# Gate and up in a macaron block: four pairs by seven products in every column group, the plain banks added by transfers, silu held back

## The chip, the cores and the metric

One core of one Trainium2 chip runs one program. The metric is device time in microseconds, from the start to the end of one execution; a kernel's time is the median of its runs. A profiled execution gives the trace: when each instruction began on each engine, how long it took and what it waited for. TensorE (PE) multiplies, VectorE (DVE) and ScalarE (ACT) work on what it reads and writes, GpSimd (POOL) issues a few transfers here, and SyncE (SP) issues the weight loads.

## The reference

The kernel computes one layer of a streaming encoder on x of 256 frames by 2048 channels, in float32. The two feed-forward half steps are where the change lies:

```python
D_MODEL = 2048; SEQ = 256; D_FF = 5504

def swiglu(h, w_gate, w_up, w_down):
    return (jax.nn.silu(h @ w_gate) * (h @ w_up)) @ w_down
...
x = x + 1/2 * SwiGLU_1(RMSNorm(x))
x = x + mixing(RMSNorm(x))     # gated DeltaNet and chunked attention, untouched here
x = x + 1/2 * SwiGLU_2(RMSNorm(x))
```

## The kernel before

**Precision.** A float32 product is made of three matmuls on halves in the type fp32r: a number is a high half (a rounded copy) plus a low half (the difference). `product` issues high by high (L455), high by low (L456) and low by high (L457) into one PSUM bank. ScalarE makes high halves by a cast, VectorE makes low halves by a subtraction.

**Column groups.** The 5504 columns of gate and up are 43 blocks of 128, taken as eleven groups of four blocks (the last has three). The groups form chunks, `CHUNKS = ((0, 4), (4, 8), (8, 11))`: after the groups of a chunk, the down projection of its blocks runs (names pd, L606 to L640). A group is named after its first block: `f1_8` is group 2 of the first feed-forward, and its banks are `pf1_8_b`. In the second feed-forward the program's names have f3, and the text calls its groups by the same numbers.

**Pairs.** The 2048 rows of a weight are 16 blocks, so eight pairs. One weight item holds one pair of gate and up columns: two 512 KB loads into a `raw` tile. A *plain* pair needs eight products, 24 matmuls: ScalarE casts it whole (`wh`, L373), VectorE subtracts (`wl`, L427). A *fast* pair, made by `begin` L389 and on, needs seven products of sums (Strassen's scheme in Winograd's form), 21 matmuls: VectorE builds four sums `s` (L399 to L401), ScalarE casts `w` and `v` (L404) and `sh` (L406), and VectorE subtracts for the low halves of `w`, `v` and `s` (L427). `fast_pairs` says which pairs are fast: none in group 0 of the first feed-forward, `FOUR = (0, 2, 4, 6)` in the first two groups of each chunk otherwise, and `FAST = (0, 2, 4)` in the rest.

**A group.** `seven` gathers the products in eight PSUM banks. Banks 1 to 4 come from one pool of four, banks 5 to 8 from another that the transposes use too. After the last fast pair, ScalarE copies bank 1 (L524) and VectorE adds banks 6, 7 and 5 (L525 to L528) into four SBUF tiles `ev`. Banks 2, 3, 4 and 8 go on and also take the plain pairs; at the end VectorE adds them to the tiles (L543), and with that they are free for the next group. `gate_up` then lets ScalarE take silu of two tiles (L559) and VectorE multiply them with the other two (L561).

**Jobs.** The result of a group is turned by TensorE (`hidden`, L138), split into halves (L128, L129) and, for some blocks, summed for the down stage (`bank_sums`, L570, L145 to L148). These jobs run at the last pair of the next group, or in the down stage for a chunk's last group.

**Down stage.** For a chunk of 16 blocks some down pairs are fast as well, and their early banks are added into the residual tiles `xd` by accumulating transfers on POOL's queue (L621). In the first chunk the fast items there are 34, 35, 37 and 38 (items are numbered in the order of their loads).

**Order.** `take_weights` and `prepare` keep weight items converted up to five products ahead (`PREP = 5`), and loads two items further. The scheduler of the tile framework puts the instructions of each engine in a fixed order. An engine runs its list in order and waits at an instruction until its operands and buffers are there. Weight tiles come from a pool named `heap`.

Of the kernel before, what the change touches and what calls it, by code (L numbers as in the profile page):

```python
# [11 lines left out]
F32 = mybir.dt.float32  # L12
F32R = mybir.dt.float32r
AF = mybir.ActivationFunctionType
ALU = mybir.AluOpType
AX = mybir.AxisListType

P = 128
T = 256
D = 2048  # L20
KD = D // P
# [8 lines left out]
FAST = (0, 2, 4)  # L30
FOUR = (0, 2, 4, 6)
# [5 lines left out]
CHUNKS = ((0, 4), (4, 8), (8, 11))  # L37
# [5 lines left out]
def block_kernel(ctx: ExitStack, tc: tile.TileContext, a: dict, out: bass.AP):  # L43
# [5 lines left out]
    nc = tc.nc  # L49
# [4 lines left out]
    sp = ctx.enter_context(tc.tile_pool(name="small", bufs=1))  # L54
# [4 lines left out]
    def heap(shape, dt, name):  # L59
        return hp.tile(shape, dt, tag="h", name=name)  # L60
# [205 lines left out]
    def fast_pairs(f, i):  # L266
        if f == "1" and i == 0:
            return ()
        return FOUR if i + (f == "1") and any(a0 <= i < a0 + 2 for a0, _ in CHUNKS) else FAST

    def pairs_of(f, i):
        return range(KD // 2) if i else FIRST if f == "1" else SECOND
# [60 lines left out]
    def by_k(w, k):  # L333

        return w.rearrange("p (c k x) -> p c k x", k=2, x=P)[:, :, k, :]
# [19 lines left out]
    def begin():  # L355


        while len(loaded) < 1 + LOAD and len(loaded) < left[0]:
            load()
        left[0] -= 1  # L360
        i, fast, pieces, raw = loaded.popleft()
        if not fast:
            out = []
            ms = [n * kk * (P if len(src.shape) == 3 else 1) for src, n, kk in pieces]
            cuts = [(slice(0, 2), ms[0])] if ms[0] == ms[1] else [(slice(at, at + 1), m) for at, m in enumerate(ms)]
            hl = [heap([P, 2, 1024], F32R, f"w{x}{i}") for x in "hl"]
            if i < 3:
                cuts = [(slice(at, at + 1), m) for at, m in enumerate(ms)]
            todo = [tuple(w[:, at, :m] for w in (*hl, raw)) for at, m in cuts]
            if i == 0:  # L370
                todo = [tuple(by_k(w[:, at], k) for w in (*hl, raw)) for at in range(2) for k in range(2)]
            for hi, _, src in todo:
                nc.scalar.copy(hi, src)  # L373
            for at, (src, n, kk) in enumerate(pieces):
                if len(src.shape) == 3:
                    n *= P
                    cols = [w[:, at, : ms[at]].rearrange("p (c k x) -> p c k x", k=kk, x=P) for w in hl]
                    cols = [[w[:, :, j, :] for j in range(kk)] for w in cols]
                else:
                    cols = [[w[:, at, j * n : (j + 1) * n] for j in range(kk)] for w in hl]  # L380
                out.append((1, (*cols, n)))
            begun.append((todo, out))
            return
        tiled = len(pieces[0][0].shape) == 3
        n = pieces[0][1] * (P if tiled else 1)
        s = heap([P, 4, n], F32, f"s{i}")
        w1 = heap([P, 2, 2 * n], F32R, f"w{i}")
        w2 = half_tile([P, 2, n], F32R, f"v{i}")

        def by_row(w):  # L390

            if tiled:
                return w.rearrange("p b (c k x) -> p b k c x", k=2, x=P)
            return w.rearrange("p b (k n) -> p b k n", k=2)

        col = lambda w: w.rearrange("p (c x) -> p c x", x=P) if tiled else w
        R = by_row(raw[:, :, : 2 * n])
        S = s.rearrange("p b (c x) -> p b c x", x=P) if tiled else s
        nc.vector.tensor_sub(S[:, 0:2], R[:, 1], R[:, :, 0])  # L399
        nc.vector.tensor_add(S[:, 2], S[:, 1], R[:, 0, 0])  # L400
        nc.vector.tensor_sub(S[:, 3], R[:, 0, 1], S[:, 2])  # L401
        parts = [(w1[:, 0], w1[:, 1], raw[:, 0, : 2 * n]), (col(w2[:, 0]), col(w2[:, 1]), R[:, 1, 1])]
        for hi, lo, src in parts:
            nc.scalar.copy(hi, src)  # L404
        sh, sl = (heap([P, 4, n], F32R, f"s{x}{i}") for x in "hl")
        nc.scalar.copy(sh, s)  # L406
        parts.append((sh, sl, s))
        k = by_row(w1)
        w11, w21 = ([k[:, s, b] for s in range(2)] for b in range(2))
        t1, t3, t2, t4 = ((sh[:, b], sl[:, b]) for b in range(4))  # L410
        w22 = (w2[:, 0], w2[:, 1])

        prods = ((1, 0, w11), (2, 2, w21), (6, 5, t2), (7, 6, t3), (4, 3, t4), (5, 4, t1), (3, 7, w22))
        begun.append((parts, [(4, prods)]))

    begun = deque()
    taken = [0]

    def prepare():
# [59 lines left out]
        return tp.tile([P, 512], F32, name=name, tag="w", bufs=8)[:, :n]  # L479


    def seven(nm, n, fast, act, jobs=(), feed=None, pairs=range(KD // 2), out=None, base=None):

        size = {b: len(fast) for b in range(1, 9)}
        for b in (2, 3, 4, 8):
            size[b] += 2 * (KD // 2 - len(fast))
        size[8] -= len(fast)
        done = dict.fromkeys(size, 0)  # L490
        banks = {}

        def add(b, act, wt):
            if b not in banks:
                banks[b] = (acc_bank if b < 5 else core_bank)(f"p{nm}_{b}")[:, :n]
            done[b] += 1
            product(banks[b], act, wt, done[b] == 1, done[b] == size[b])

        ev = {}
        idle = 0  # L500
        for at_pair, j in enumerate(pairs):
            if j in fast:
                ps = take_weights()
                for at, (b, i7, w) in enumerate(ps):
                    add(b, act(j, i7), w)
                    if at == 3:
                        tick()
            else:
                for s in range(2):
                    wh, wl, _ = take_weights()  # L510
                    if feed and s == 0:
                        feed(at_pair)
                    for k, w in enumerate(zip(wh, wl)):
                        for t in range(2):
                            add((2, 4, 3, 8)[2 * s + t], act(j, 2 * k + t), w)
                    idle += 1
                    if idle > 3 and jobs and j > max(fast, default=-1):
                        jobs.popleft()()
                    while at_pair == KD // 2 - 1 and s == 1 and jobs:
                        jobs.popleft()()  # L520
            if fast and j == fast[-1]:
                idle = 1
                g0, u0, g1, u1 = (wide(f"e{nm}_{x}", n) for x in range(4))
                nc.scalar.copy(g0, banks[1])  # L524
                nc.vector.tensor_add(u0, banks[6], g0)  # L525
                nc.vector.tensor_add(g1, banks[7], u0)
                nc.vector.tensor_add(u1, banks[5], g1)
                nc.vector.tensor_add(u0, banks[5], u0)  # L528
                ev = {2: g0, 3: u0, 4: g1, 8: u1}
                if base:  # L530
                    for b, x in base.items():
                        nc.vector.tensor_add(ev[b], x, ev[b])
        if out:
            for b, put in out.items():
                put(ev[b])
                e = wide(f"e{nm}_{b}", n)
                nc.scalar.copy(e, banks[b])
                put(e)
            return None
        if not fast:  # L540
            return banks
        for b in (2, 3, 4, 8):
            nc.vector.tensor_add(ev[b], banks[b], ev[b])  # L543
        return ev

    def gate_up(nm, f, i, xr, jobs, feed):

        c, m = FG[i]
        n, fast = m * P, fast_pairs(f, i)
        src = seven(f"f{nm}_{c}", n, fast, xr.sums_of, jobs, feed, pairs_of(f, i))  # L550
        if not fast:
            banks = src
            src = {b: wide(f"e{nm}_{c}_{b}", n) for b in QUAD}
            for b in QUAD:
                (nc.scalar.copy if b % 4 else nc.vector.tensor_copy)(src[b], banks[b])
        gs = [src[b] for b in (2, 4)]
        us = [src[b] for b in (3, 8)]
        for t in range(2):
            nc.scalar.activation(gs[t], src[(2, 4)[t]], AF.Silu, scale=xr.rn[:, t : t + 1])  # L559
        for t in range(2):  # L560
            nc.vector.scalar_tensor_tensor(  # L561
                us[t], src[(3, 8)[t]], xr.half_rn[:, t : t + 1], gs[t], op0=ALU.mult, op1=ALU.mult
            )
        return us

    def bank_sums(ps, more, nm):
# [655 lines left out]
    act = xr2.more_again(DOWN)  # L1222
# [16 lines left out]
    for d in range(4):  # L1239
        pss = pair(f"pwa{d}")  # L1240
        gemm(pss, H, quads(oa), 512)
        for t in range(2):
            cs = slice(512 * d, 512 * (d + 1))
            s = wide(f"wa{d}{t}")
# [7 lines left out]
    for d in (0, 2):  # L1252
        ev = seven(f"wo{d}", 512, DOWN, block, base=residual(d, "wo"))
# [89 lines left out]
```

## Time and profile before

| | |
|---|---|
| median of 3 runs | 2105.24 us (2103.96 to 2107.07) |
| profiled execution | 2104.86 us, its span 2103.1 us |
| granted TensorE clock | 0.999 |
| TensorE, VectorE, ScalarE, POOL busy | 2086.8, 1798.9, 1190.7, 64.5 us |
| first feed-forward's groups 0, 1, 2, 3 end at | 60.1, 100.9, 144.2, 186.6 us |
| its first down stage ends at | 272.0 us |
| second feed-forward's groups 0, 1, 2, 3 end at | 1456.1, 1496.9, 1540.2, 1582.7 us |

A group's end is the end of the last matmul into its bank 8. Matmuls overlap in TensorE's pipeline, so that the time listed for one is longer than the distance between two starts. Busy shares are of the span.

### The profile page before, as it was taken

What the parts mean: (1) busy time and instruction counts of PE and PEld (TensorE: products, weight loads), DVE (VectorE), ACT (ScalarE), POOL (GpSimd) and SP (SyncE); (2) the same over time, 40 slices, a digit from 0 to 9 for tenths busy, and PEclk for the clock granted to TensorE, in tenths of its full rate; (3) what the DMA queues carried; (4) which work ended last, traced back from release to release, by engine and by line L of the source; (5) the groups of instructions that cost most, each with busy time, mean ns of one, the idle gap of its engine ahead of it and who ended that gap; (6) DMA issues with size and microseconds to landing.
All of it is one profiled execution on the core that took longest, in us unless ns stands there. A gap on an engine that the chain in (4) does not pass through costs nothing.

```text
span 2103.1 us, 25704 instructions
## 1 busy us (share of the span) xinstructions
PE 2086.8 (99%) x9732; PEld 1743.5 (83%) x9732; DVE 1798.9 (86%) x2015; ACT 1190.7 (57%) x1226; POOL 64.5 (3%) x77
## 2 busy tenths in 40 slices
PE   8999999999999999999999999999999999999999
PEld 6888888878898988888888888888887888878897
DVE  6998999989996688767785787999999999989982
ACT  6755565646555555557545555556555555556561
POOL 0000110002000000000010000000000100011000
PEclk9999999999999999999999999999999999999999
DMA  9655995649866656435454466767665975579581
GB/s 314 218 188 177 261 266 196 207 145 278 257 212 219 238 187 224 163 127 197 145 175 159 151 200 220 230 203 228 207 193 169 276 243 192 180 207 294 188 271 60
DMA packets 398204, 434.59 MB, mean 207 GB/s; under 512 B 14704, under 2 KB 372352, under 8 KB 397824
## 3 DMA queue, kind: packets, MB, share of 16 engines
q1 hardware_dynamic: 388864, 416.17, 60.8%
q0 software_dynamic: 9216, 16.78, 4.5%
q8 instruction: 76, 1.25, 0.3%
q14 instruction: 48, 0.39, 0.1%
HBM read 407.72 MB, written 25.17 MB: 206 GB/s over the span
## 4 chain that ended last, share of the span: by engine, by line
PE 95%; DVE 2%; SPq 1%; issue 1%; DMA 0%; ACT 0%; DVEq 0%; ACTq 0%
PE pf L455 14%; PE pf L457 14%; PE pf L456 14%; PE pd L456 7%; PE pd L457 7%; PE pd L455 7%; PE pg L456 2%; PE pg L457 2%; PE pg L455 2%; PE pc L455 2%; PE pc L457 2%; PE pc L456 2%; PE pwo L455 1%; PE pwo L457 1%; PE pwo L456 1%; DVE wl L427 1%
## 5 line engine op out<-in xcount | busy, mean ns | idle before, releaser
L427 DVE TENSOR_TENSOR wl<-raw,wh 128x2048 fp32r<-128x2048 f32 (+5 forms) x278 | 587.2, 2120 | 69.6 <-PE pc L456 17.0
L373 ACT CAST wh<-raw 128x2048 fp32r<-128x2048 f32 (+5 forms) x278 | 490.2, 1779 | 95.3 <-DVE wl L427 18.3
L406 ACT CAST sh<-s 128x2048 fp32r<-128x2048 f32 (+1 forms) x123 | 233.0, 1894 | 292.5 <-DVE s L401 288.4
L427 DVE TENSOR_TENSOR sl<-s,sh 128x2048 fp32r<-128x2048 f32 (+1 forms) x123 | 276.9, 2257 | 27.3 <-PE pd L456 12.0
L456 PE MATMUL pf<-wl,xr 128*128 128x512 f32 (+1 forms) x704 | 271.4, 386 | 0.2 <-DVE wl L427 0.2
L457 PE MATMUL pf<-wh,xr 128*128 128x512 f32 (+1 forms) x704 | 271.0, 385 | 0.0
L455 PE MATMUL pf<-wh,xr 128*128 128x512 f32 (+1 forms) x704 | 263.3, 387 | 3.9 <-ACT xr L180 2.4
L457 PE MATMUL pd<-wh,hid 128*128 128x512 f32 x432 | 169.1, 391 | 0.0
L456 PE MATMUL pd<-wl,hid 128*128 128x512 f32 x432 | 168.3, 390 | 0.0
L404 ACT CAST w<-raw 128x1024 fp32r<-128x1024 f32 (+1 forms) x123 | 128.0, 1041 | 65.4 <-DVE sl L427 12.8
L455 PE MATMUL pd<-wh,hid 128*128 128x512 f32 x432 | 163.6, 392 | 0.0
L455 PEld LDWEIGHTS pf<-wh,xr 128*128 128x128 f32 x704 | 132.4, 188 | 30.3 <-ACT wh L373 2.9
L427 DVE TENSOR_TENSOR w<-raw,w 128x1024 fp32r<-128x1024 f32 (+1 forms) x123 | 148.1, 1204 | 10.4 <-ACT w L404 10.2
L399 DVE TENSOR_TENSOR s<-raw 128x1024 f32<-128x1024 f32 (+1 forms) x123 | 147.9, 1202 | 7.1 <-PE pg L456 4.6
L456 PEld LDWEIGHTS pf<-wl,xr 128*128 128x128 f32 x704 | 132.6, 188 | 25.3 <-DVE wl L427 0.5
L457 PEld LDWEIGHTS pf<-wh,xr 128*128 128x128 f32 x704 | 132.6, 188 | 25.3
L404 ACT CAST v<-raw 128x512 fp32r<-128x512 f32 (+1 forms) x123 | 75.6, 615 | 97.0 <-PE pf L457 32.3
L456 PE MATMUL pf<-sl,xf 128*128 128x512 f32 (+1 forms) x292 | 112.3, 385 | 0.0
L457 PE MATMUL pf<-sh,xf 128*128 128x512 f32 (+1 forms) x292 | 112.0, 385 | 0.0
L455 PE MATMUL pf<-sh,xf 128*128 128x512 f32 (+1 forms) x292 | 110.2, 386 | 0.0
L621 POOL DMA_DIRECT2D xd<-ed x64 | 56.0, 996 | 1305.5 <-ACT ed L524 1225.5
L457 PEld LDWEIGHTS pd<-wh,hid 128*128 128x128 f32 x432 | 81.1, 188 | 17.2
(509 smaller groups left out, 4270.5 us busy)
## 6 DMA issues: line engine op xcount, KB each, us to landing
raw<-wd SPq DMA_DIRECT2D x168, 512.0 KB, 5.2
raw<-wg SPq DMA_DIRECT2D x159, 512.0 KB, 3.8
raw<-wu SPq DMA_DIRECT2D x159, 512.0 KB, 5.3
raw<-wgt SPq DMA_DIRECT2D x64, 512.0 KB, 4.6
raw<-wa SPq DMA_DIRECT2D x48, 512.0 KB, 4.6
raw<-wc SPq DMA_DIRECT2D x48, 512.0 KB, 4.7
xd<-ed POOLq DMA_DIRECT2D x64, 256.0 KB, 7.0
raw<-wbr SPq DMA_DIRECT2D x32, 512.0 KB, 5.2
```

Of the source, the lines that this page charges most:

```text
L373: nc.scalar.copy(hi, src)
L399: nc.vector.tensor_sub(S[:, 0:2], R[:, 1], R[:, :, 0])
L404: nc.scalar.copy(hi, src)
L406: nc.scalar.copy(sh, s)
L427: nc.vector.tensor_sub(lo, src, f32(hi))
L455: nc.tensor.matmul(dst, ah, wh, start=start, stop=False)
L456: nc.tensor.matmul(dst, ah, wl, start=False, stop=False)
L457: nc.tensor.matmul(dst, al, wh, start=False, stop=stop)
L621: b: lambda e, dst=xd[d + dd][t]: nc.gpsimd.dma_start(dst, e, accum_op=ALU.add)
```

## The change

Three things change in gate and up. All groups use four fast pairs, except group 0 of the first feed-forward (none, as before) and group 0 of the second (three, as before): ten pairs become fast, in groups 2, 3, 6, 7 and 10 of each feed-forward. In every fast group that isn't the last of its chunk (15 groups), the four additions of L543 are replaced: ScalarE copies the banks to a heap tile `es`, and four accumulating transfers on POOL's queue add it to the tiles. And in these groups silu and the multiplication are put off until the `sh` cast of the second fast item prepared after that. A tile `gate` orders them: it is filled by POOL, read by that cast as its bias, and then holds the copy of the scales that silu reads.

```diff
     def fast_pairs(f, i):
         if f == "1" and i == 0:
             return ()
-        return FOUR if i + (f == "1") and any(a0 <= i < a0 + 2 for a0, _ in CHUNKS) else FAST
+        return FOUR if i + (f == "1") else FAST
...
         sh, sl = (heap([P, 4, n], F32R, f"s{x}{i}") for x in "hl")
-        nc.scalar.copy(sh, s)
+        ready_now = []
+        for job in held:
+            job[0] -= 1
+        while held and held[0][0] <= 0:
+            ready_now.append(held.popleft())
+        if ready_now:
+            nc.scalar.activation(sh, s, AF.Identity, bias=ready_now[0][1][:, 0:1])
+        else:
+            nc.scalar.copy(sh, s)
+        for _, _, job in ready_now:
+            job()
...
+        if spill:
+            es = heap([P, 4, n], F32, f"e{nm}")
+            for i, b in enumerate((2, 4, 3, 8)):
+                nc.scalar.copy(es[:, i], banks[b])
+                nc.gpsimd.dma_start(ev[b], es[:, i], accum_op=ALU.add)
+            return ev
         for b in (2, 3, 4, 8):
             nc.vector.tensor_add(ev[b], banks[b], ev[b])
...
+        spill = bool(fast) and all(i != a1 - 1 for _, a1 in CHUNKS)
...
+        def turn_held():
+            rn = gate_tile()
+            nc.scalar.copy(rn, xr.rn)
+            gated(rn)        # silu on ScalarE, the multiplication on VectorE
+        if spill:
+            hold = gate_tile()
+            nc.gpsimd.memset(hold, 0.0)
+            held.append([2, hold, turn_held])
+        else:
+            gated(xr.rn)
```

In the changed kernel the lines have moved: products are L471 to L473, the `sh` cast is L415 or, with the gate, L413, subtractions are L443, the copies to `es` L561, the transfers L562, the memset L597, silu L584, the multiplication L586.

The first place is the end of group 2 of the first feed-forward, on ScalarE. Before, the hidden casts of group 1 (L128), its bank sums' copies (L570) and silu of group 2 (L559) stand among the casts of items 25 to 28:

```order
L128 CAST hid1_1_928<-hid1_1_928_0_0_1165 128x2x256
L570 COPY shid1_1_928_0_1172<-hid1_1_928_0_0_1165 128x128
L128 CAST hid1_1_928<-hid1_1_928_2_0_1192 128x2x256
L128 CAST hs1_12_929<-shid1_1_928_0_1172 128x512
L404 CAST w26_1223<-raw26_1105 128x1024
L570 COPY shid1_1_928_2_1199<-hid1_1_928_2_0_1192 128x128
L406 CAST sh26_1230<-s26_1222 128x2048
L128 CAST hs1_12_929<-shid1_1_928_2_1199 128x512
L559 ACTIVATE ef1_8_0_1089<-ef1_8_0_1089,rn1_106 128x512
L373 CAST wh27_1287<-raw27_1132 128x2048
L559 ACTIVATE ef1_8_2_1091<-ef1_8_2_1091,rn1_106 128x512
```

Now the four copies out of the banks stand there, behind the hidden casts and the first cast of `hs`:

```order
L415 CAST sh26_1216<-s26_1208 128x2048
L128 CAST hid1_1_931<-hid1_1_931_0_0_1232 128x2x256
L128 CAST hid1_1_931<-hid1_1_931_2_0_1247 128x2x256
L607 COPY shid1_1_931_0_1239<-hid1_1_931_0_0_1232 128x128
L607 COPY shid1_1_931_2_1254<-hid1_1_931_2_0_1247 128x128
L128 CAST hs1_12_932<-shid1_1_931_0_1239 128x512
L561 COPY ef1_8_1262<-pf1_8_2_937 128x512
L561 COPY ef1_8_1262<-pf1_8_4_949 128x512
L561 COPY ef1_8_1262<-pf1_8_3_957 128x512
L128 CAST hs1_12_932<-shid1_1_931_2_1254 128x512
L561 COPY ef1_8_1262<-pf1_8_8_1000 128x512
```

Silu of group 2 has moved down. It stands behind item 30, whose `sh` cast reads the gate; the list goes on like this, with what each instruction waits for:

```order
L404 CAST w28_1328<-raw28_1205 128x1024 [waits DMAHW5_49,DVE_49,Activation_49]
L415 CAST sh28_1335<-s28_1327 128x2048 [waits DMASW5_49,DMASW6_49,DMASW4_49,DMASW7_49,DVE_49,Activation_49]
L373 CAST wh29_1376<-raw29_1303 128x2048 [waits DMAHW0_49,DMASW3_49,DMAHW7_49,DMASW2_49,Activation_49]
L404 CAST v30_1399<-raw30_1324 128x512 [waits DMAHW2_49,PE_49]
L404 CAST w30_1398<-raw30_1324 128x1024 [waits DMAHW1_49]
L413 ACTIVATE sh30_1405<-s30_1397,gate_1271 128x2048 [waits DVE_49,Activation_49,Pool_49]
L373 CAST wh31_1451<-raw31_1373 128x2048 [waits DMAHW4_49,DMAHW3_49,PE_49]
L592 COPY gate_1408<-rn1_106 128x2 [waits Activation_49]
L584 ACTIVATE ef1_8_0_1175<-ef1_8_0_1175,gate_1408 128x512 [waits Activation_49]
```

The cast of item 28 has come to stand behind the four transfers (DMASW4 to DMASW7), which before it did not; item 30 is a fast item now.

The second place is TensorE at the start of group 3, whose banks are `pf1_12_b`. Before:

```order
L457 MATMUL pf1_8_8_997<-wh23_1101,xr1_5_196 128x512
L455 MATMUL pf1_12_1_1256<-w24_1109,xf1_0_277 128x512
L456 MATMUL pf1_12_1_1256<-w24_1109,xf1_0_277 128x512
L457 MATMUL pf1_12_1_1256<-w24_1109,xf1_0_277 128x512
L455 MATMUL pf1_12_2_1260<-w24_1109,xf1_0_277 128x512
L456 MATMUL pf1_12_2_1260<-w24_1109,xf1_0_277 128x512
```

Now, from the last of the eight transposes of group 1's result, which stand between the groups:

```order
L138 MATMUL hid1_1_931_2_0_1247<-cst_103,ef1_4_3_852 128x128
L471 MATMUL pf1_12_1_1275<-w24_1131,xf1_0_277 128x512
L472 MATMUL pf1_12_1_1275<-w24_1131,xf1_0_277 128x512
L473 MATMUL pf1_12_1_1275<-w24_1131,xf1_0_277 128x512
L471 MATMUL pf1_12_6_1283<-sh24_1138,xf1_0_277 128x512
L472 MATMUL pf1_12_6_1283<-sl24_1139,xf1_0_277 128x512
L473 MATMUL pf1_12_6_1283<-sh24_1138,xf1_0_277 128x512
L471 MATMUL pf1_12_1_1275<-w26_1209,xf1_2_314 128x512
L472 MATMUL pf1_12_1_1275<-w26_1209,xf1_2_314 128x512
L473 MATMUL pf1_12_1_1275<-w26_1209,xf1_2_314 128x512
L471 MATMUL pf1_12_6_1283<-sh26_1216,xf1_2_314 128x512
L471 MATMUL pf1_12_7_1287<-sh24_1138,xf1_0_277 128x512
```

Bank 2 was the second product of the group; now products into banks 1, 6 and 7, of two items, come before it (three more rows into bank 7 follow before `pf1_12_2`).

The third place is VectorE in the first down stage, at the sums of its fast item 37. Before:

```order
L427 TENSOR_TENSOR v37_1693<-raw37_1542,v37_1693 128x512
L129 TENSOR_TENSOR hs1_25_1255<-shid1_3_1579_0_1615,hs1_25_1255 128x512
L399 TENSOR_TENSOR s37_1691<-raw37_1542 128x1024
L427 TENSOR_TENSOR w37_1692<-raw37_1542,w37_1692 128x1024
L400 TENSOR_TENSOR s37_1691<-s37_1691,raw37_1542 128x512
L401 TENSOR_TENSOR s37_1691<-raw37_1542,s37_1691 128x512
```

Now:

```order
L399 TENSOR_TENSOR s37_1723<-raw37_1552 128x1024
L129 TENSOR_TENSOR hs1_25_1274<-shid1_3_1611_0_1647,hs1_25_1274 128x512
L400 TENSOR_TENSOR s37_1723<-s37_1723,raw37_1552 128x512
L443 TENSOR_TENSOR w37_1724<-raw37_1552,w37_1724 128x1024
L401 TENSOR_TENSOR s37_1723<-raw37_1552,s37_1723 128x512
```

The operations are the same; the subtraction for `v37` now stands a few rows further ahead and the first sum one row earlier.

More of the change, by code (lines that the diff above doesn't have):

```diff
@@ L416, in block_kernel, with gate_tile @@
     begun = deque()
+    held = deque()
+    def gate_tile():
+        return sp.tile([P, 2], F32, name="gate", tag="gate", bufs=1)
     taken = [0]
@@ L479, in wide, with seven @@
         return tp.tile([P, 512], F32, name=name, tag="w", bufs=8)[:, :n]
-    def seven(nm, n, fast, act, jobs=(), feed=None, pairs=range(KD // 2), out=None, base=None):
+    def seven(nm, n, fast, act, jobs=(), feed=None, pairs=range(KD // 2), out=None, base=None, spill=False):
         size = {b: len(fast) for b in range(1, 9)}
@@ L549, in gate_up @@
         n, fast = m * P, fast_pairs(f, i)
-        src = seven(f"f{nm}_{c}", n, fast, xr.sums_of, jobs, feed, pairs_of(f, i))
+        spill = bool(fast) and all(i != a1 - 1 for _, a1 in CHUNKS)
+        src = seven(f"f{nm}_{c}", n, fast, xr.sums_of, jobs, feed, pairs_of(f, i), spill=spill)
         if not fast:
@@ L557, in gate_up, with gated @@
         us = [src[b] for b in (3, 8)]
[L558 to L563, printed above, removed]
+        def gated(rn):
+            for t in range(2):
+                nc.scalar.activation(gs[t], src[(2, 4)[t]], AF.Silu, scale=rn[:, t : t + 1])
+            for t in range(2):
+                nc.vector.scalar_tensor_tensor(
+                    us[t], src[(3, 8)[t]], xr.half_rn[:, t : t + 1], gs[t], op0=ALU.mult, op1=ALU.mult
+                )
+        def turn_held():
[8 more added lines that the diff above has]
+            gated(xr.rn)
         return us
```

## The prediction

> **What bounds the kernel now.** I read first the page (busy shares, the clock, the chain), then who TensorE waits for, then the stretches between the ends of column groups, then the order of time around the places that the change touches. The page:
>
> ```profile
> PE 2086.8 (99%) x9732; PEld 1743.5 (83%) x9732; DVE 1798.9 (86%) x2015; ACT 1190.7 (57%) x1226; POOL 64.5 (3%) x77
> PEclk9999999999999999999999999999999999999999
> PE 95%; DVE 2%; SPq 1%; issue 1%; DMA 0%; ACT 0%; DVEq 0%; ACTq 0%
> ```
>
> TensorE is busy for 99% of the span at full clock and carries 95% of the chain. So time falls only if TensorE has less to do, and rises only if TensorE is made to wait. VectorE is second, and it is not far behind. The stretches from group end to group end (columns: PE, PEld, DVE, ACT, POOL busy, clock, DMA share, GB/s), groups 1, 2 and 3 of the first FFN and its first down stage:
>
> ```profile
> 60.10:100.90 40.80, 40.80 (x182) 33.71 (x181) 40.29 (x46) 27.12 (x28) 0.00 (x0) 1.00 0.74 239
> 100.90:144.20 43.30, 43.30 (x200) 35.99 (x199) 41.71 (x49) 25.22 (x25) 0.00 (x0) 1.00 0.52 170
> 144.20:186.60 42.40, 42.40 (x192) 35.13 (x191) 38.28 (x35) 23.15 (x22) 0.00 (x0) 1.00 0.63 198
> 186.60:229.90 43.30, 42.37 (x190) 34.30 (x190) 39.57 (x45) 23.98 (x25) 2.74 (x3) 1.00 0.60 182
> ```
>
> In group 3 TensorE fills 42.40 us and VectorE 38.28 of them: 4.1 us of slack. Only in the down stage does TensorE (42.37 of 43.30) stand still. Where it does is in the list of waits and in the order of time (total, times, longest; then start, duration):
>
> ```profile
> PE pd L455 <- ACT sh L406: 3.7, 4, 0.9
> ```
>
> ```profile
> 209.16 0.39 PE L456 MATMUL pd<-w,hid 128*128 128x512 f32 x1
> 209.39 0.39 PE L457 MATMUL pd<-w,hid 128*128 128x512 f32 x1
> 210.71 0.74 PE L455 MATMUL pd<-sh,hs 128*128 128x512 f32 x2 [0.93 <-ACT sh L406]
> ```
>
> Starts of neighbouring matmuls lie 0.23 us apart although each lists 0.39: they overlap, so 0.227 is what one costs. The gap from 209.39 to 210.71 is 1.32, of which 1.09 is lost. This happens four times, at the third fast item (37 in the first chunk) of each down stage of 16 blocks, which I call the entry: 4.4 us in all. VectorE made the operand late:
>
> ```profile
> 207.61 0.69 DVE L401 TENSOR_TENSOR s<-raw,s 128x512 f32<-128x512 f32 x1
> ...
> 208.76 1.90 ACT L406 CAST sh<-s 128x2048 fp32r<-128x2048 f32 x1
> ```
>
> **The change part by part.** *Ten pairs lose a product* (groups 2, 3, 6, 7, 10 of each FFN): 24 matmuls become 21, so 24 of 128x512 and six of 128x384 go. The narrow ones start 0.17 apart:
>
> ```profile
> 630.16 0.33 PE L455 MATMUL pf<-wh,xf 128*128 128x384 f32 x1
> 630.33 0.33 PE L456 MATMUL pf<-wl,xf 128*128 128x384 f32 x1
> ```
>
> That is 24 x 0.227 + 6 x 0.17 = 6.5 us of TensorE work, 0.68 per wide pair. (By the listed 0.39 it would be twice that; the starts decide.)
>
> *VectorE*: a pair of eight costs one wl of 2.28; a pair of seven costs these:
>
> ```profile
> 153.45 1.21 DVE L399 TENSOR_TENSOR s<-raw 128x1024 f32<-128x1024 f32 x1
> 154.58 1.21 DVE L427 TENSOR_TENSOR w<-raw,w 128x1024 fp32r<-128x1024 f32 x1
> 155.72 0.68 DVE L400 TENSOR_TENSOR s<-s,raw 128x512 f32<-128x512 f32 x1
> 156.32 0.68 DVE L427 TENSOR_TENSOR v<-raw,v 128x512 fp32r<-128x512 f32 x1
> 156.92 0.68 DVE L401 TENSOR_TENSOR s<-raw,s 128x512 f32<-128x512 f32 x1
> 157.53 2.28 DVE L427 TENSOR_TENSOR wl<-raw,wh 128x2048 fp32r<-128x2048 f32 x1
> 159.73 2.28 DVE L427 TENSOR_TENSOR sl<-s,sh 128x2048 fp32r<-128x2048 f32 x1
> ```
>
> By spacing the five of the pair before wl take 153.45 to 157.53, 4.08, and sl (2.2) takes the place of wl (2.2): +4.08 a pair, some +39 for the ten with the narrow ones. Against it 60 of the bank adds go:
>
> ```profile
> 146.99 1.88 DVE L543 TENSOR_TENSOR ef<-pf,ef 128x512 f32<-128x512 f32 x3
> ```
>
> ```profile
> L543 DVE TENSOR_TENSOR ef<-pf,ef x84: 545/679/692, 99.7 to 2034.5; 128x512 f32<-128x512 f32 x76, 128x384 f32<-128x384 f32 x8
> ```
>
> Three in 1.8 is 0.60 each, so 36 us go. VectorE comes out about even in total. By place it does not: groups 1, 4, 5, 8, 9 (and 0 of the second FFN) get 2.4 lighter, groups 2 and 6 get 1.7 heavier, groups 3 and 7 (no transfers there) 4.08 heavier, or 2.3 counting the three adds of the group before that ran inside them (146.99 above). Slack of 4.1 covers that.
>
> *ScalarE* takes 60 copies out of PSUM and ten more w, v and sh in place of wh:
>
> ```profile
> L524 ACT COPY ef<-pf x21: 479/578/589, 91.6 to 2017.6; 128x512 f32<-128x512 f32 x19, 128x384 f32<-128x384 f32 x2
> ```
>
> ```profile
> 100.88 1.03 PE L138 MATMUL hid<-cst,e 128*128 128x128 f32 x8
> ...
> 101.09 1.91 ACT L406 CAST sh<-s 128x2048 fp32r<-128x2048 f32 x1
> ...
> 102.91 1.06 ACT L128 CAST hid<-hid 128x512 fp32r<-128x512 f32 x2
> ```
>
> 60 x 0.58 = 35, plus about 1.5 a pair: 50 us on an engine 57% busy; nothing by itself. But the copies now release the PSUM banks, and they stand on ScalarE behind casts. Next group's TensorE needs bank 2 first. Ends of first groups of a chunk: copies come in time, 0. Ends of second groups: after eight transposes and some nine matmuls there is just room, except after group 1 of the first FFN, where in the new order an sh cast (1.91), two hid casts and the copy stand in a row. Started at 101.57, that row ends at 104.95; TensorE gets to bank 2 at 104.03: **0.9 lost**. Ends of groups 2 and 6 (four places): hid casts, bank sums and an hs cast stand ahead; I reckon the last copy 4.6 us after the group's end, and TensorE has eight transposes (1.03) and fourteen matmuls (3.2), so some 0.5 lost each. Bounds for one boundary: 0 (the copy first) to 1.9 (one more cast ahead).
>
> *POOL* issues 60 transfers of 256 KB and 15 memsets of two columns. The nearest rows are the down stage's (issue min/median/max in ns, then landing):
>
> ```profile
> L621 POOL DMA_DIRECT2D xd<-ed x64: 862/865/1579, 223.1 to 1925.6; - x64
> ...
> DMA to landing us min/median/max: 4.1/7.0/9.6
> ```
>
> The queue is empty there, so it hides the issuing (60 us on an engine 3% busy). Bytes: 60 x 256 KB beside 434 MB is 4%, on DMA engines at 0.52 to 0.74 in these stretches: nothing. SP's loads stay as they are.
>
> *Silu is held.* Its multiply moves some 15 us later; its reader, the transposes, runs only at the end of the next group, 42 us later: nothing. The new wait is another one: in ScalarE's new order, the second sh cast after the end of group 2 (item 28) waits until the four transfers have landed. Copies at T+4.6 with T = 144.2, four issues of 0.996 mean, the last started at T+7.7, landing 7.0 later: T+14.7. Before, that cast began at T+13.5, and TensorE came to it at T+21.8:
>
> ```profile
> 157.69 1.92 ACT L406 CAST sh<-s 128x2048 fp32r<-128x2048 f32 x1 [5.24 <-DVE s L401]
> ...
> 165.97 0.39 PE L455 MATMUL pf<-sh,xf 128*128 128x512 f32 x1
> 166.19 0.39 PE L456 MATMUL pf<-sl,xf 128*128 128x512 f32 x1
> ```
>
> A cast at 14.7 ends at 16.6, sl at 18.9; TensorE wants sl at 22.0. Cost 0; queued behind it are wh casts and VectorE's sl, 1.2 us later. Bounds: landing at 4.1 (no wait) to 9.6 (3.8 later).
>
> The Trainium skill, "DMA: Bandwidth & Descriptors", section "Anatomy of one DMA — SWDGE (gpsimd) path", fits 2.0 us plus bytes over 436 GB/s, an estimate of 2.6 us for 256 KB. This trace has 7.0 in the median and 4.1 at least, so it disagrees; by the page the held cast would not wait at all, and the chance of the slow rival below would halve.
>
> *The down entry.* Walking the new order with these durations from the end T of group 2 (or 6), the sh cast that TensorE waited for ends at T+66.0, against T+66.5 before. Bounds: the wait of 1.09 disappears altogether (TensorE would then come through at T+64.7), or the 2.3 more of VectorE work are all exposed (T+68.8). I take 66.0, nearest to the rows walked; it also swallows the 0.5 bank wait ahead of it and group 3's own 0.68.
>
> Sum: pairs of groups 2 and 6, 4 x 0.68 = 2.7; entries, 4 x 0.5 = 2.0; groups 10, 6 x 0.17 = 1.0; bank wait after group 1, -0.9. **4.8 us faster**: the profiled execution, 2104.86, becomes 2100.1. It stands 0.4 under the median of the runs (2105.24), so the median becomes 2100.4. What a measurement of this kernel can tell from no change is 0.2%, 4.2 us.
>
> **The rivals.**
>
> *A: bank waits eat it.* The copies lose 0.5 at each of the ten other boundaries as well, where my walk leaves 0 to 0.6 of room: +4.5, so 2105, no change. For: TensorE needs the bank within 1.6 to 2.3 us and ScalarE's casts are 1.9 long. Against: ScalarE is idle nearly half the time.
>
> *B: the landing decides, slower.* Issues of 1.58 and landings of 9.6, both seen, put the gate at T+4.6+4.7+9.6 = T+18.9, 5.4 later than now. TensorE would still get sh at T+20.8 but sl only at T+23.0, and VectorE would be 5.4 late with 1.8 us of slack left (4.1 - 2.3): about 3 us later at each entry in place of 0.5 earlier, 4 x 3.0 = 12 against the other terms (-2.7 - 1.0 + 0.9): 2114. It is slower by more than 4.2 once an entry comes 1.75 later, the gate then 4.1 late: a landing of 9.9 us with issues of 0.996, or of 8.1 with issues of 1.58. For: VectorE sits at the edge at each entry. Against: 7.0 median with the DMA engines busier than in groups.
>
> *C: VectorE holds up POOL's issuing.* If each issue had to wait out one 2.28 us operation, the last would start 9.1 later: gate at T+23.8, sl at T+28, 6 us after TensorE wants it at T+22.0, at four places: 24 - 2.8, 2126. The median issue of 865 ns is also nearly the least, 862, while VectorE was busy for 91% (39.57 of 43.30): so not seen here. The Trainium skill, "SBUF — State Buffer", section "Who interferes with whom", has VectorE and GpSimd share ports by an exclusive lock, VectorE with two SBUF inputs against GpSimd's reads; by these rows the lock does not hold up the issues.
>
> *D: the entry waits vanish.* VectorE, lighter in groups 0 and 1, arrives early at the entries: 4 x 1.3 = 5 more: 2095.5.
>
> **How the numbers follow.** Likeliest 0.52 (2098 to 2103.5); A 0.22; B 0.14; C 0.02; D 0.10. Of the likeliest, centred 0.6 beyond the bound of 4.2, I count 0.37 as faster and 0.15 as the same. Faster: 0.37 + 0.10 = 0.47. Same: 0.15 + A's 0.22 = 0.37. Slower: B and C, 0.16. The range goes from 2095.5 (D) over A to 2108, where an entry comes 1.4 later than now; it leaves out about 0.12 of B and C above and 0.05 below.
>
> **What would show it.** Right: 30 fewer matmuls in gate and up at 0.227 apart; VectorE's L543 group down to 24; ScalarE's copies behind hid casts, TensorE's waits on them short and at the ends of groups 1, 2, 6; the gated cast of sh starting near T+15; the wait at pd on sh between 0 and 1 us. Wrong: TensorE waits on copies at most boundaries (A), landings of the new transfers beyond 9 us with waits at pd of 3 us (B), POOL issues of several us (C), no wait at pd (D).

## The result and the profile after

The changed kernel is slower. Its median is 2119.53 us (2117.36 to 2123.26) against 2105.99 for the kernel before in the same sessions: ratio 1.0065, 95% interval 1.0053 to 1.0078, 13.5 us. The forecast was 2100.4, with a range up to 2108.0 and a chance of 0.16 for slower. The profiled execution shown here took 2123.26 us, the slowest of four.

The page after, the same rows as before:

```profile
PE 2090.1 (99%) x9702; PEld 1737.2 (82%) x9702; DVE 1803.1 (85%) x2005; ACT 1237.8 (58%) x1321; POOL 119.3 (6%) x152
...
PEclk9999999999999999999999999999999999999999
...
PE 21%; DVE 3%; DMA 2%; issue 1%; ACT 1%; POOL 0%; SPq 0%; DVEq 0%; ACTq 0%; POOLq 0%
```

There are 30 matmuls fewer (9702 for 9732), and VectorE's sum is the same as before to 4 us, as forecast. The chain's shares add up to 28% only: the page could follow it back over no more than that end of the span, and in that part it leaves TensorE for transfers and VectorE. What TensorE waited for (total, times, longest):

```profile
PE pd L471 <- DVE ef L565: 5.8, 6, 2.1
PE pd L471 <- ACT sh L415: 4.4, 4, 1.1
PE pd L472 <- DVE wl L443: 2.9, 4, 1.6
PE pf L471 <- DVE shid L148: 2.8, 4, 1.3
PE pf L471 <- ACT xr L180: 2.4, 1, 2.4
PE pf L471 <- ACT ef L561: 2.3, 2, 1.5
```

The second row is the old wait at the down entries, a little longer. The first and third are new and lie in the down stages; the first is the start of each of the six down stages, where TensorE needs the banks of the chunk's last group and VectorE has not yet added them. The fourth and sixth are waits for banks at the starts of groups. The stretches of group 3 and of the first half of the down stage (the same columns as in the prediction):

```profile
143.80:186.40 42.60, 42.34 (x189) 34.27 (x188) 36.46 (x42) 26.59 (x29) 3.63 (x5) 1.00 0.77 222
186.40:235.00 48.60, 45.38 (x197) 36.21 (x196) 43.12 (x49) 24.36 (x26) 2.77 (x4) 0.96 0.55 164
```

VectorE had 2.3 us more to do in group 3 (the pair less the adds) and did less in it, 36.46 for 38.28. It stood still for 6.1 us there, 3.13 of them in one wait, and had to catch up in the down stage, which took 5.3 us longer. The order of time says why: ScalarE's copies out of the banks, then the cast of item 28; VectorE behind it; POOL's issues.

```profile
147.71 1.55 ACT L561 COPY ef<-pf 128x512 f32<-128x512 f32 x3
...
160.18 1.91 ACT L415 CAST sh<-s 128x2048 fp32r<-128x2048 f32 x1 [6.33 <-DMA ef<-ef]
```

```profile
156.70 2.29 DVE L443 TENSOR_TENSOR wl<-raw,wh 128x2048 fp32r<-128x2048 f32 x1
162.12 2.29 DVE L443 TENSOR_TENSOR sl<-s,sh 128x2048 fp32r<-128x2048 f32 x1 [3.13 <-ACT sh L415]
...
190.16 0.68 DVE L565 TENSOR_TENSOR ef<-pf,ef 128x512 f32<-128x512 f32 x1
```

```profile
L562 POOL DMA_DIRECT2D ef<-ef x4: 862/1382/1563, 148.6 to 150.6; - x4
...
DMA to landing us min/median/max: 3.4/6.6/9.5
```

The first issue came at 148.6, 4.7 us after the group's end at 143.9: as forecast. But the four land one behind the other, 3.4, 5.5, 7.7 and 9.5 us after their own issue, that is 2.7 us apart, the last at 160.1. The cast of item 28 starts at 160.18, when it has. VectorE idles 3.13 us, and the add that frees bank 2 (L565) ends at 190.84, for a TensorE that had been waiting 2.1 us:

```profile
191.00 0.47 PE L471 MATMUL pd<-wh,hid 128*128 128x512 f32 x1 [2.13 <-DVE ef L565]
...
192.70 0.63 PE L471 MATMUL pd<-wh,hid 128*128 128x512 f32 x1
193.13 0.63 PE L472 MATMUL pd<-wl,hid 128*128 128x512 f32 x1
```

Soon after that wait, from 192.2 on, matmuls start 0.43 apart instead of 0.23 for 3.4 us: TensorE's granted clock (third column from the right) is 0.50 there, and 1.7 us are lost.

```profile
192.20:195.50 3.30, 3.30 (x9) 2.54 (x8) 3.30 (x5) 2.52 (x2) 0.00 (x0) 0.50 0.12 37
```

Item 28 is not alone. Other tiles got the buffers of copied banks too, and ScalarE's casts and SyncE's weight loads wait for landings at more places (total, times, longest):

```profile
ACT wh L373 <- DMA ef<-ef: 26.8, 7, 4.7
...
ACT sh L415 <- DMA ef<-ef: 25.7, 4, 6.6
```

```profile
SPq L350 <- DMA ef<-ef: 44.9, 8, 11.9
```

### The profile page after: what moved, and what is told of

It reads as the page before. It is cut to its first block, busy times and chain, and to the rows that moved or that the text cites. A ratio compares the mean times of both kernels' runs of the same rounds, so it can differ in the third digit from the quotient of the medians.

```text
span 2121.5 us, 25948 instructions
## 1 busy us (share of the span) xinstructions
PE 2090.1 (99%) x9702; PEld 1737.2 (82%) x9702; DVE 1803.1 (85%) x2005; ACT 1237.8 (58%) x1321; POOL 119.3 (6%) x152
## 3 DMA queue, kind: packets, MB, share of 16 engines
q8 instruction: 76, 1.25, 0.3%
## 5 line engine op out<-in xcount | busy, mean ns | idle before, releaser
L443 DVE TENSOR_TENSOR wl<-raw,wh 128x2048 fp32r<-128x2048 f32 (+5 forms) x268 | 566.3, 2120 | 65.7 <-PE pc L472 16.9
L373 ACT CAST wh<-raw 128x2048 fp32r<-128x2048 f32 (+5 forms) x268 | 473.9, 1779 | 111.2 <-DMA ef<-ef 26.8
L415 ACT CAST sh<-s 128x2048 fp32r<-128x2048 f32 (+1 forms) x118 | 223.4, 1893 | 260.6 <-DVE s L401 230.6
L443 DVE TENSOR_TENSOR sl<-s,sh 128x2048 fp32r<-128x2048 f32 (+1 forms) x133 | 299.1, 2254 | 36.8 <-ACT sh L415 13.2
L471 PE MATMUL pf<-wh,xr 128*128 128x512 f32 (+1 forms) x704 | 267.6, 386 | 3.9 <-ACT xr L180 2.4
L473 PE MATMUL pf<-wh,xr 128*128 128x512 f32 (+1 forms) x704 | 271.3, 385 | 0.0
L443 DVE TENSOR_TENSOR w<-raw,w 128x1024 fp32r<-128x1024 f32 (+1 forms) x133 | 160.2, 1205 | 27.8 <-ACT w L404 26.8
L471 PE MATMUL pd<-wh,hid 128*128 128x512 f32 x432 | 165.8, 397 | 5.8 <-DVE ef L565 5.8
L473 PE MATMUL pd<-wh,hid 128*128 128x512 f32 x432 | 169.3, 392 | 0.0
L399 DVE TENSOR_TENSOR s<-raw 128x1024 f32<-128x1024 f32 (+1 forms) x133 | 160.0, 1203 | 9.7 <-DMA raw<-wu 5.0
L404 ACT CAST w<-raw 128x1024 fp32r<-128x1024 f32 (+1 forms) x133 | 137.9, 1037 | 51.6 <-DVE sl L443 17.7
L471 PEld LDWEIGHTS pf<-wh,xr 128*128 128x128 f32 x704 | 132.5, 188 | 30.2 <-ACT xr L180 2.8
L473 PEld LDWEIGHTS pf<-wh,xr 128*128 128x128 f32 x704 | 132.5, 188 | 25.2 <-DVE xr L181 0.2
L471 PE MATMUL pf<-sh,xf 128*128 128x512 f32 (+1 forms) x332 | 126.1, 387 | 2.8 <-DVE shid L148 2.8
L473 PE MATMUL pf<-sh,xf 128*128 128x512 f32 (+1 forms) x332 | 127.5, 384 | 0.0
L472 PE MATMUL pf<-sl,xf 128*128 128x512 f32 (+1 forms) x332 | 127.4, 384 | 0.0
L471 PEld LDWEIGHTS pd<-wh,hid 128*128 128x128 f32 x432 | 81.5, 189 | 24.8 <-issue 6.8
L472 PEld LDWEIGHTS pd<-wl,hid 128*128 128x128 f32 x432 | 81.6, 189 | 22.4 <-DVE wl L443 6.3
```

The lines of the kernel that those rows point to most:

```text
L443: nc.vector.tensor_sub(lo, src, f32(hi))
L471: nc.tensor.matmul(dst, ah, wh, start=start, stop=False)
L472: nc.tensor.matmul(dst, ah, wl, start=False, stop=False)
L473: nc.tensor.matmul(dst, al, wh, start=False, stop=stop)
```

## The experiments

Theory 1: the wait for the landing, which reaches ScalarE because the pool gives the buffer of the copied banks (`es`) to the next tile that needs one. Theory 2: VectorE's load in a chunk's last group. All ratios are to the kernel before, with 95% intervals.

**Keep the buffer (keep_es).** A tiny instruction after the held silu reads `es`, so its buffer is given out later:

```diff
...
             gated(rn)
+            keep = sp.tile([P, 2], F32, name="keep", tag="keep", bufs=1)
+            nc.scalar.activation(keep, gs[0][:, 0:2], AF.Identity, bias=es[:, 0, 0:1])
...
```

> The changed kernel, with one thing added: after the held silu a tiny ScalarE instruction reads a column of the copied banks (es), so that the pool gives es's buffer to another tile only after that, and the sh cast of item 28 and its like no longer wait for the four transfers to land. Theory 1 (the landing): those waits (25.7 us on ScalarE's sh casts, 3.1 us of idle VectorE each in groups 3 and 7) are what makes VectorE late at the end of the chunk; without them TensorE's waits at the start of pd on the bank adds (5.8 us) and on wl (2.9) go, and the time falls from 2119.5 by 8 to 12 us, to some 2108 to 2111. Theory 2 (the load): VectorE is late because a chunk's last group has 4.08 us more of its work; the waits at pd stay, and the time stays within 2 us of the changed kernel.

Measured: 2108.99 us, ratio 1.0016 (1.0007 to 1.0025). ScalarE's cast of item 28 now starts at 157.19, and what stays of TensorE's waits is:

```profile
157.19 1.92 ACT L415 CAST sh<-s 128x2048 fp32r<-128x2048 f32 x1 [3.03 <-PE pf L474]
```

```profile
PE pd L472 <- ACT sh L415: 4.4, 4, 1.1
PE pd L473 <- DVE wl L444: 2.9, 4, 1.7
...
PE pf L472 <- DVE shid L148: 1.1, 4, 0.3
...
PE pf L472 <- ACT ef L563: 0.8, 1, 0.8
```

The wait on the bank adds is gone altogether. Between the two kernels lie 0.5% or 10 us: theory 1's number. The transfers still land as late as before; only nobody waits for them: the waits of the sh casts, of the wh casts and of the loads are gone together, so the 10 us are for all three, and item 28's share of them is not shown by itself. The waits on wl did not go, against theory 1: they are another thing.

**Fast pairs as before, transfers kept (spill_only).** `FOUR` only in the first two groups of each chunk. Here the silu of groups 2 and 6 of both feed-forwards, and of group 9 of the first, comes after the transposes that should read it, and that of group 9 of the second is left out (two silu and two multiplications); apart from these the work is the same.

> The transfers and the held silu as in the changed kernel, but the fast pairs as before (three in groups 2, 3, 6, 7, 10). The sh cast of item 28 and its like still wait for the landing. Theory 1 (the landing): VectorE is late at the down stages all the same, so slower than before by 4 to 8 us, 2110 to 2114. Theory 2 (the load): VectorE has 36 us less to do than before, so no waits at the start of pd, and apart from the waits for the banks that ScalarE now copies (some 5 us in the changed kernel) nothing is lost: 2104 to 2107.

Measured: 2116.60, ratio 1.0054 (1.0041 to 1.0066): slower than both theories said, with 35 us less work for VectorE than before. TensorE waits on the copies out of the banks for 4.3 us, one of these waits being followed by 3.4 us at a granted clock of 0.50, and its waits on sh in pd are what they were before (3.7 listed). The sh casts still wait for landings (23.2 us in four), yet the wait on the bank adds at the starts of the down stages is gone. So theory 2 alone does not explain the loss, and theory 1 missed another part, the late copies.

**Four pairs, no transfers (four_only).** `spill = False`.

> Four fast pairs everywhere as in the changed kernel, but no transfers and no held silu: VectorE adds the banks, as before. VectorE then has 39 us more to do than before and ScalarE does not copy. Theory 1 (the landing): no transfer is waited for, but VectorE needs some 42.6 us for a group of TensorE's 41.7, so it falls behind by the end of each chunk: 2112 to 2120. Theory 2 (the load): as much as in the changed kernel and 2.4 us a group more: 2120 to 2130.

Measured: 2116.85, ratio 1.0051 (1.0039 to 1.0064). Without the relief the pairs overload VectorE: TensorE waits 6.6 us on sh in the groups and 3.7 on wl in pd. Theory 1's number, and what the transfers are there for.

**Three pairs in groups 3 and 7 (no_last).** Here too the silu of groups 2 and 6 comes after the transposes that should read it.

> The changed kernel with three fast pairs in groups 3 and 7 of both feed-forwards, as before: the four pairs just ahead of the deep down stages are plain again (TensorE 2.7 us more work, VectorE 4.08 us less in each of these groups). The wait of item 28's cast for the landing stays. Theory 1 (the landing): VectorE still loses 3 us there, but has 4.08 us more room, so half or more of the loss at pd goes: 2108 to 2113. Theory 2 (the load): all of the loss at pd goes; what stays are the waits for the copied banks: 2104 to 2108.

Measured: 2110.38, ratio 1.0024 (1.0014 to 1.0034). Item 28's cast still waits for the landing, yet TensorE's wait on the bank adds has all but gone:

```profile
159.89 1.91 ACT L415 CAST sh<-s 128x2048 fp32r<-128x2048 f32 x1 [6.37 <-DMA ef<-ef]
```

```profile
PE pd L471 <- ACT sh L415: 3.7, 4, 0.9
PE pf L471 <- ACT ef L561: 2.9, 2, 2.1
...
PE pd L471 <- DVE ef L565: 0.4, 1, 0.4
```

Theory 1's number, but it says more: the late start of a down stage needs both, the landing and the 4.08 us. Either taken away, most of the loss goes.

**Two transfers instead of four (two_spill).**

```diff
-            for i, b in enumerate((2, 4, 3, 8)):
+            for b in (3, 8):
+                nc.vector.tensor_add(ev[b], banks[b], ev[b])
+            for i, b in enumerate((2, 4)):
```

> The changed kernel with two transfers a group in place of four: ScalarE copies banks 2 and 4 and they are added by transfer, VectorE adds banks 3 and 8 as before. Nothing keeps es's buffer longer. In the changed kernel the four transfers of a group land one behind the other (after 3.4, 5.5, 7.7, 9.5 us at the end of group 2). Theory 1 (the buffer comes free when the last of a queue of four has landed): two land by some 5.5 us, so the sh cast of item 28 no longer waits, although VectorE has 1.2 us more to do in each of 15 groups: 2109 to 2114. Theory 2 (VectorE's load in the chunk's last group): with more load it gets worse than the changed kernel: 2120 to 2125.

Measured: 2110.39, ratio 1.0019 (1.0010 to 1.0028), theory 1's number. VectorE has more to do than in the changed kernel, and the time is 9 us shorter. The waits on the bank adds shrink (3.5 us in 3), they do not vanish; nor did the landing cease to matter, as expected: item 28's cast no longer waits for it, but at three later places the sh casts still do, 16.3 us for 25.7 in four.

**Kept buffer, three pairs in groups 3 and 7 (keep_no_last).** The silu is held for one fast item in groups 2 and 6.

> The kernel that keeps es's buffer until after the silu (2109.0), with three fast pairs in groups 3 and 7, as before; the silu of groups 2 and 6 is held for one fast item, not two. If what is left there is VectorE's load in the chunk's last group, TensorE's waits in pd on wl (2.9 us listed, 3.5 lost) go and the four waits on sh shrink from 1.25 to 1.09, 4.1 in all, for 2.7 more of TensorE's work: 2107 to 2108. If it is the copied banks and the transposes' banks, the waits in pd stay and 2.7 comes on top: 2111 to 2112.

Measured: 2110.88 (2106.84 to 2117.58), ratio 1.0024 (1.0014 to 1.0033): neither number clearly, and a wide spread. The waits on wl in pd fell from 2.9 to 1.7 and those on sh to 3.7, but one new wait of 2.3 on ScalarE (ed L554) came. Inconclusive by itself.

**Copies first (keep_first).** With the buffer kept, the jobs of the group before are issued after the copies:

```diff
-                    while at_pair == KD // 2 - 1 and s == 1 and jobs:
+                    while at_pair == KD // 2 - 1 and s == 1 and jobs and not spill:
...
                 nc.gpsimd.dma_start(ev[b], es[:, i], accum_op=ALU.add)
+            while jobs:
+                jobs.popleft()()
```

> The kernel that keeps es's buffer (2109.0), with the transposes of the group before issued behind the copies out of the banks, so that on ScalarE the copies stand ahead of the hidden casts and the bank sums. If the waits at the start of a group (1.0 after group 1, 0.4 each at four starts of group 3 and 7) come from the copies' place on ScalarE, they go: 2106 to 2107.5. If they come from the banks that transposes and bank sums hold, the sums are now later and the waits stay or grow: 2109 to 2111.

Measured: 2104.18 (2103.83 to 2106.99), ratio 0.9992 (0.9983 to 1.0001): more than expected. The waits at the starts of groups are gone:

```profile
PE pd L472 <- ACT sh L415: 4.4, 4, 1.1
PE pd L473 <- DVE wl L444: 2.7, 4, 1.6
PE pf L472 <- ACT xr L180: 2.4, 1, 2.4
```

The copies' place on ScalarE behind the hidden casts and bank sums was the other part, worth some 5 us.

**Both (keep_first_no_last).**

> Both edits together: copies ahead of the hidden casts, and three fast pairs in groups 3 and 7. If each of the two causes is what it is taken for, their gains add up: 2104.5 to 2106.5, the same as before within what can be measured, with 18 matmuls fewer (3.8 us of TensorE's work, of which one wait of 1.0 to 1.7 or so is left to account for). If not, 2108 to 2112.

Measured: 2103.70, ratio 0.9990 (0.9981 to 0.9999). The best of all, 0.1% faster than before, which is at the edge of what can be told. The gains add up in part: the waits in pd on wl fall to 1.3 in one, on sh to 3.7.

**Copies first, buffer not kept (first_only).**

> The changed kernel with the copies out of the banks ahead of the transposes of the group before, and nothing that keeps es's buffer. In its order the sh cast of item 28 no longer waits for the transfers (the pool gives es's buffer to a later item), while the load of item 23 and two w casts still wait for a landing. If the two mechanisms found (the wait for the landing through the buffer, the banks freed late) are all that made the changed kernel slow: within 1.5 us of the kernel with both edits, 2103 to 2106. If keeping the buffer itself matters at other places: 2107 to 2112.

Measured: 2128.60, ratio 1.0103 (1.0090 to 1.0117). A clear miss, above even the second number, and the most telling one. Item 28 no longer waits, but the pool now gives `es`'s buffer to others. Early in groups 6 and 10 of both feed-forwards a w cast of ScalarE waits for a landing, up to 10.4 us; VectorE stands behind it and TensorE behind VectorE:

```profile
ACT w L404 <- DMA ef<-ef: 32.2, 4, 10.4
```

```profile
368.86 1.05 ACT L404 CAST w<-raw 128x1024 fp32r<-128x1024 f32 x1 [8.70 <-DMA ef<-ef]
```

```profile
372.89 2.28 DVE L443 TENSOR_TENSOR wl<-raw,wh 128x2048 fp32r<-128x2048 f32 x1
```

```profile
375.23 0.50 PE L472 MATMUL pf<-wl,xr 128*128 128x512 f32 x1 [3.03 <-DVE wl L443]
```

```profile
PE pf L472 <- DVE wl L443: 13.0, 6, 4.1
```

Behind three of these four waits the granted clock is 0.50 for 13.7 us in all, which costs up to 6.8 us. The loads on SyncE's queue wait for landings as well, 39.3 us in eight, but so they do in the changed kernel (44.9); they are not what is new here.

So the cost is not tied to item 28: it falls on whichever tile gets the buffer, and on everything queued behind it.

**Transfers without the pairs (keep_first_three).** Kept buffer, copies first, pairs as before; the silu is held for one fast item where the next group has three.

> Transfers, kept buffer and copies first, but the fast pairs as before: the transfers alone, without their two waits. VectorE has 36 us less to do than before, TensorE the same. If VectorE's lateness at the down entries (4 waits, 4.4 us) comes from its load in the groups ahead, they shrink by half or more: 2101 to 2104. If the entries are set within the down stage itself (each sum waits for its raw load and buffer there), they stay 1.1 each: 2105 to 2107.

Measured: 2107.82 (2104.93 to 2111.09), ratio 1.0006 (0.9997 to 1.0015). With VectorE 33 us lighter the entry waits are 3.7 us listed, four times, as before to the digit: a lighter VectorE in the groups does not shrink them. ScalarE's wait ahead of the v cast of item 37 is the same here as before and as in keep_first_no_last; the rows are of these two:

```profile
202.76 0.62 ACT L404 CAST v<-raw 128x512 fp32r<-128x512 f32 x1 [2.01 <-PE pd L457]
```

```profile
201.53 0.62 ACT L404 CAST v<-raw 128x512 fp32r<-128x512 f32 x1 [2.01 <-PE pd L474]
```

**The changed kernel again (after_again).**

> The changed kernel once more, on the same chip as the others and with a profile of its own: 2117 to 2121. The stretch of ten matmuls at 0.43 us apart after the wait at the first down stage (2.0 us lost) need not recur: it followed a gap of 2.5 us between two starts; with a gap below 2.2 the profile should show none there and the time should be 2 us less.

Measured: 2120.94, ratio 1.0065 (1.0051 to 1.0080). The gap before 190.87 was as long as before, 2.6 us from start to start, against the condition written down, and no slow stretch followed:

```profile
190.87 0.47 PE L471 MATMUL pd<-wh,hid 128*128 128x512 f32 x1 [2.22 <-DVE ef L565]
191.17 0.39 PE L472 MATMUL pd<-wl,hid 128*128 128x512 f32 x1
```

The span was 2119.2 for 2121.5. The first profile has a second such stretch, at 21.5 near its start, which the profile before has too and this one has not: together they cost 3.4 us, 1.7 each and not the 2.0 expected, which is more than the difference.

**More half buffers, one heap tile less (half4).** On keep_first_no_last: `NB = 21`, `NH = 4`.

> The best kernel so far (kept buffer, copies first, three fast pairs in groups 3 and 7: 2103.7) with four buffers for the v halves in place of two, and one heap tile fewer (21), which leaves SBUF's use as it was. At the entry of the down stage ScalarE's v cast of item 37 waits for TensorE (2.01 us before it, the same in the kernel before and in this one), since both v buffers are in use. If that is what sets the four entry waits (1.09 each), they shrink or go: 2099.5 to 2102. If it is something else (the sums' order on VectorE, the raw loads), they stay, and the smaller heap costs something: 2104 to 2110.

Measured: 2195.54, ratio 1.0427 (1.0409 to 1.0445), far outside both numbers, some 90 us. The loads come late everywhere (ScalarE waits 109 us on those of up where it casts v, in 49 places), and TensorE's waits are followed by stretches at a granted clock of 0.50, 61 us in all, which is up to some 30 us of the loss. What sets the entry waits remains open; that they go with more v buffers could not be seen. The edit changes two pools; that the late loads come from the smaller heap is likely and not shown.

## Why the prediction was wrong, point by point

*TensorE's 6.5 us.* Right. Where two matmuls start more than 0.227 us apart, the excess adds up to 40.2 us in keep_first and to 35.5 before, while its profiled execution is 1.0 us shorter (2103.84 for 2104.86): 4.7 us more of standing still and yet 1.0 less, so 5.7 of the 6.5 can be seen.

*VectorE even in total.* Right (1803.1 for 1798.9). four_only shows that the pairs alone overload it.

*The gated cast, "Cost 0".* This is the step that failed. The first issue was forecast right (T+4.7 for T+4.6) and the last came even earlier (T+6.7 for T+7.7); the landing was not, 9.5 us for 7.0, so that the cast began at T+16.3 and not at T+14.7. The 7.0 was the median of all transfers of the down stage, whatever was ahead of them, where the last of four was asked for. The trace before had a case: of three issued there 0.5 us apart the landings are 7.2, 8.4 and 9.6.

```profile
L621 POOL DMA_DIRECT2D xd<-ed x3: 862/1213/1564, 275.3 to 276.3; - x3
...
DMA to landing us min/median/max: 7.2/8.4/9.6
```

And "cost 0" looked at TensorE's need of sl alone. The 1.2 us written as queued behind it were 3.13 us of idle VectorE, in the very group that has 4.08 us more work. The other casts and the loads that wait for a landing were not in the prediction at all.

*The entry at T+66.0.* Wrong. A lighter VectorE in the groups left the four entry waits as they were (keep_first_three), so the 0.5 to win is not borne out. With four pairs in groups 3 and 7 each grew from 1.09 to 1.25 (in two_spill at three of the four places), and in the first chunk of the changed kernel the cast ended at T+71.7, after all that TensorE had lost ahead of it. What VectorE's lateness moved was a wait that the prediction did not have: the start of the down stage, on the last group's bank adds, 5.8 us in six. The waits on wl, 2.9, come later in the stage and stay when nobody waits for a landing.

*Bank waits.* After group 1 of the first feed-forward 1.0 was lost (forecast 0.9). But the same happened at other group ends, up to 1.7, where the walk left "0", and behind group 2 the last copy ended at T+6.4, where the walk had T+4.6; in all some 5 us, by keep_first against keep_es. Rival A was thus right as to place, its price (4.5) too, beside and not instead of B.

*Rival B, 0.14, 2114.* It named the landing and VectorE's late arrival in the down stage. Its threshold, a gate 4.1 us late, was too high: the gate came 2.8 late (T+16.3 for T+13.5), and that was enough, since the bank adds at the start of the down stage, which it did not have, come due ahead of the entry. The evidence was in the prediction (a longest landing of 9.6 us, a longest issue of 1.58) and was taken for a tail, when it was the price of a transfer with others ahead of it. C is out: the first issue takes 862 ns; the later ones are listed with more, but they start before the ones ahead have ended, and their ends lie 0.9 us apart.

*The price of one transfer.* The Trainium skill, "DMA: Bandwidth & Descriptors", section "Anatomy of one DMA — SWDGE (gpsimd) path", would give 2.6 us for each of these, an estimate from its fixed and per-byte cost. The first of a burst landed after 3.4, the fourth after 9.5; the measurement decides.

The sum, from the changed kernel back: between the forecast and the measurement lie 13.5 + 4.8 = 18.3 us. Of these 10 are the waits for the buffer and 5 the copies' place, as two runs show. The rest, some 3 us, goes with waits in the down stages, listed as 7.1 us in keep_first and 3.7 before. That four pairs in groups 3 and 7 cost them is borne out by keep_first_no_last, which has 2.7 us more of matmuls and is no slower; how one leads to the other stays open.

## What to carry to other kernels

A transfer that replaces an engine's work holds its source buffer until it lands: ask who gets that buffer next and what is queued behind that, and price the landing of the last of a burst on one queue, not of one transfer alone. Moving the release of a PSUM bank to another engine moves it behind that engine's list; put the copy ahead of the work that isn't urgent. Where a step uses up the slack of the second-busiest engine and another one delays it, check the two together at the next place where the first engine waits for it, not only at the places that waited before.

## What the runs showed of the hardware

Four accumulating transfers of 256 KB, SBUF to SBUF, issued 0.5 to 0.9 us apart on POOL's queue, landed one behind the other: 3.4, 5.5, 7.7, 9.5 us after their issues, up to 11.8 at other places.

After a gap between two starts TensorE's granted clock can fall to 0.50 for 3.41 us, in which matmuls of 128x512 start 0.43 us apart. In the fourteen profiles here it did so after 17 of 30 gaps of 2.26 to 2.79 us, after all twelve longer ones, and after none of 2.0 to 2.25: in the changed kernel's first profile after 2.52 us, in its second not after 2.61. (One such stretch, in half4, had no gap of that size ahead of it.) The Trainium skill, "TensorE: Matmul & The Clock Gate", section "Part 1: The HAM clock gate (the "warmup" mystery)", has a half-speed clock after an idle window of some 3.4 us; the spacing agrees, but here gaps of 2.3 to 2.5 us were followed by it in the profiles of six of these kernels, and the measurement decides.
